# ConvFFN up projection: the summed weight blocks of Strassen's product are formed by adding DMAs instead of by vector instructions, with signs turned

## The chip, the core and the metric

The kernel runs on one core of a Trainium2 chip. Five engines work beside each other, each through its own list of instructions in order: TensorE (PE, matrix products), VectorE (DVE), ScalarE (ACT), GpSimd (POOL) and SyncE (SP, which here only issues DMAs). They wait for each other and for DMAs through semaphores. All DMAs of the core share 16 DMA engines. The metric is the device time of one execution in microseconds (us), as the median over runs.

## The reference

Two decoder layers over 1024 tokens of width 1024. Layer 0 mixes tokens by gated linear attention and layer 1 by native sparse attention, both beside attention to a memory; each layer ends in a ConvFFN. The change lies in the ConvFFN, whose inner width is 2816:

```python
def conv_ffn(h, w_up, conv_w, conv_b, w_down):
    T = h.shape[1]
    a, b = jnp.split(h @ w_up, 2, axis=-1)
    a_pad = jnp.pad(a, ((0, 0), (CONV_WIDTH - 1, 0), (0, 0)))
    a = sum(a_pad[:, j:j + T] * conv_w[j] for j in range(CONV_WIDTH)) + conv_b
    return (jax.nn.silu(a) * b) @ w_down
...
x = x + conv_ffn(rmsnorm(x, g_ffn[l]), w_up[l], conv_w[l], conv_b[l], w_down[l])
```

## The kernel before

Everything is kept transposed: channels on the 128 partitions, tokens along the free dimension. A float32 operand of a product is split into a rounded high part (ACT copies it, `split`, L1022) and a low part, the difference (DVE, L1023). Each product then takes three matmuls (high by high, high by low, low by high: L1058, L1059, L1060).

**Units.** The up projection of a layer is cut into 22 units (`class Up`). Unit i makes 128 channels of the convolved branch a and the same 128 channels of the gate b. Its weights are four blocks of 128 x 512 float32, 256 KB each: block(j, k) with j = 0 for a and 1 for b, and k the half of the 1024 inputs. Called A00, A01, A10, A11 below. The right-hand side, the normalised stream, is also cut into two halves of channels by two halves of 512 tokens. A unit is thus a 2 x 2 by 2 x 2 block product, made by Strassen's scheme (in Winograd's form) with seven products instead of eight. The products are named 1 to 7 (`p1` to `p7`), and each takes 4 x 3 = 12 matmuls of 128 x 128 by 512 columns.

**Left operands.** Products 1, 2 and 4 take A00, A01 and A11 as they are (`direct`). The other four take sums (`sums`, L1042 to L1045): S1 = A10 + A11 for product 5, S3 = A00 - A10 for 7, S2 = S1 - A00 for 6, and S4 = A01 - S2 for 3. For the four first units of a layer these sums run on DVE, for the 18 others on POOL. They are written in place, into the two raw tiles that the four blocks were loaded into (`load`, L1019), and then split by `split67` and `split35`, two blocks to an instruction.

**Right operands.** `blocks1` makes the sums and differences of the normalised stream (L591, L592, L598, L599) once per layer; `h_d` holds one block for later.

**Results.** Products 1, 2 build X (the first token half of a); ACT copies product 1 to s1. Product 6 opens the PSUM bank Y, and DVE reads it at once into q (`opened`, L1092); product 7 adds to the same bank, and DVE reads it into t (`drained`, L1097); product 4 adds to it again (L1106). So PE may start product 7 only when q has been read, and product 4 only when t has been read. Products 5 and 3 use the bank W. The convolution is ACT's L1117 followed by DVE's L1119 and L1123 (called taps below), the gate is a product with silu on DVE, and `mixed` forms the sums that the down projection needs of the gated values (L1147). They are stored to `gb_d`.

**Order.** Per layer: units 0 and 1 run as a pair beside the end of the output projection. Units 2 to 5 are "early" units: their products 1 and 2 are made ahead from separately loaded weights (`pre`) and kept in DRAM, so that they have only products 6, 7, 5, 4, 3 left. After the pair the order is 6, 2, 7, 3, 8, 4, 9, 5 and then 10 to 21: late and early units in turn, later late units alone. `run(u, last, then, after)` writes one step: the products of u, the convolution of the unit before it, the splits of the next unit, the loads of the one after. A scheduler in the framework then sets each engine's order from this. On an early unit's step the product 1 of the next unit is made too, so that in the alternating part every step has six products.

**Buffers.** Four raw tiles of 128 x 1024, two per unit; six tiles for split operands ("wrl") and four pairs for the others ("Ah", "Al").

**Down projection.** `add_x` and the last products add its result to the stream x (L1377, L1465).

Of the kernel before, what the change touches and what calls it, by code (L numbers as in the profile page):

```python
# [14 lines left out]
P = 128  # L15
# [19 lines left out]
def kernel(  # L35
# [543 lines left out]
    def blocks1(norm, gc, B):  # L579
        rs = norm.done()  # L580
        yield "norm"
        lo, hi = xs[:4], xs[4:]
        a, b = hs(0), hs(1)
        tt = nc.vector.tensor_tensor

        for r in (7, 6, 5, 4, 3):
            B[r] = []
        for j in range(4):
            scaled_x(1, rs, gc, (j, 4 + j))
            nc.sync.dma_start(h_d[j], hi[j][:, b])  # L590
            tt(lo[j][:, b], hi[j][:, b], lo[j][:, b], ALU.subtract)  # L591
            tt(lo[j][:, a], lo[j][:, b], lo[j][:, a], ALU.add)  # L592
# [386 lines left out]
    def ffn(l, blocks_, after):  # L979
# [8 lines left out]
        def slot(what, n, make):  # L988
            if what not in ring:
                ring[what] = [make() for _ in range(n)]  # L990
                turn[what] = 0
            turn[what] += 1
            return ring[what][turn[what] % n]

        turn = {}

        def either(n):
            if "A" not in ring:
                ring["A"] = [(V(F32R, "Ah"), V(F32R, "Al")) for _ in range(2)]
            return ring["A"][n]  # L1000

        def raws():
            return [wp.tile([P, 1024], F32, tag="raw", name=nm("wu"), bufs=4) for _ in range(2)]

        class Up:
# [5 lines left out]
            def load(self, k=None):  # L1011
                if k is None:
                    self.load(0)
                    k = 1
                if k == 0:
                    self.raw = slot("raw", 2, raws)
                t = self.raw[k]
                for j in (1, 0) if self.early else (0, 1):
                    nc.sync.dma_start(t[:, hs(j)], w_up[l, j * NF + self.i, :, hs(k)])  # L1019
# [9 lines left out]

            def direct(self):  # L1030
                t = slot("one", 2, lambda: wrl("A"))
                hi, lo = t[:, hs(0)], t[:, hs(1)]
                if self.early:
                    self.split((4,), self.raw[1][:, hs(1)], hi, lo)
                else:
                    self.split((1,), self.raw[0][:, hs(0)], hi, lo)
                    self.split((2, 4), self.raw[1], *slot("two", 2, lambda: (wrl("Ah"), wrl("Al"))))

            def sums(self):
                (a0, b0), (a1, b1) = ((t[:, hs(0)], t[:, hs(1)]) for t in self.raw)  # L1040
                tt = (nc.vector if self.soon else nc.gpsimd).tensor_tensor
                tt(b1, b0, b1, ALU.add)  # L1042
                tt(b0, a0, b0, ALU.subtract)
                tt(a0, b1, a0, ALU.subtract)
                tt(a1, a1, a0, ALU.subtract)  # L1045

            def split67(self, past=None):
                self.split((6, 7), self.raw[0], *either(self.i == 1), past)

            def split35(self, past=None):  # L1050
                self.split((3, 5), self.raw[1], *either(self.i != 0), past)
# [136 lines left out]
        def ahead(then, after):  # L1188
            if after is not None:
                after.load(1)  # L1190
            if then is not None and then.early:
                then.again()

        def run(u, last, then, after):
            nxt = [then] if then is not None else []
            if u.s1 is None:
                u.p1()
            u.p6()
            if after is not None:
                after.load(0)  # L1200
            if u.early:
# [3 lines left out]
                u.split35((then.kept, u.opened))  # L1205
# [23 lines left out]
            mix(u.ended)  # L1229
            u.p3()  # L1230
# [8 lines left out]
        for n, u in enumerate(seq):  # L1239
            u.n, u.mate = n // 2, seq[n - 1] if n % 2 else None  # L1240
            u.soon = n < 4
        each(pair, "load", "direct")
# [4 lines left out]
        each(pair, "sums")  # L1247
# [3 lines left out]
        each(pair, "split67", "p6", "p7")  # L1251
        next(rest)
        each(pair, "act0", "split35", "p5")
# [6 lines left out]
        then.sums()  # L1260
        each(pair, "p3")
        then.split67()
# [155 lines left out]
        def down():  # L1418
# [40 lines left out]
            for t0, w in segs_:  # L1459
                c = slice(t0, t0 + w)  # L1460
                for m in range(4):
# [3 lines left out]
                    tt(xv, bank[m][:, c], xv, ALU.add)  # L1465
# [560 lines left out]
```

## Time and profile before

| | |
|---|---|
| median of 3 runs | 2257.14 us (2255.66 to 2258.51) |
| span of the profiled execution | 2257.4 us; no other time of this execution is given |
| PE busy | 2215.0 us, 98% |
| DVE busy | 1729.8 us, 77% |
| ACT busy | 1126.3 us, 50% |
| POOL busy | 433.6 us, 19%, of it 212.0 us in the sums L1042 to L1045 |
| DMA | 285.15 MB, mean 126 GB/s |

The page gives busy time per engine, the chain that ended last, and groups of instructions with the idle time in front of them. PE's share alone tells that there is little idle time to win; where the 42 us lie in which PE is idle, the windows and the table of waits tell. Times in the rows are from the start of the span; layer 0's up projection stands at about 400 to 840 us, layer 1's at about 1630 to 2030 us.

### The profile page before, as it was taken

The page shows a single profiled execution, that of the slowest core. Times are in us where ns is not written, and L with a number is a line of the kernel's source. Part 1 is how long each engine was busy: PE and PEld are TensorE (multiplying, and loading weights), DVE is VectorE, ACT ScalarE, POOL GpSimd, SP SyncE. Part 2 cuts the span into 40 slices and gives each one's busy share as a digit, 9 for nine tenths or more (in the row PEclk, how much of TensorE's full clock was granted, in tenths as well). Part 3 has the DMA queues.
Part 4 walks back from the last instruction along what each step waited for, and adds up shares of the span by engine and source line. Part 5 has one row for each costly group of instructions (what it writes and reads, how often), then busy time and mean ns, then how long its engine had stood idle before and what let it go on. Part 6 is the DMA issues. An engine that isn't in the chain of part 4 may idle for free.

```text
span 2257.4 us, 31218 instructions
## 1 busy us (share of the span) xinstructions
PE 2215.0 (98%) x10994; PEld 1826.2 (81%) x10994; DVE 1729.8 (77%) x3069; ACT 1126.3 (50%) x2085; POOL 433.6 (19%) x409
## 2 busy tenths in 40 slices
PE   9999999999999999999999999999999999999997
PEld 7888887777888888888888878778777788888886
DVE  6786886888877768887756778866988877768877
ACT  5464464543333335456544788864543333334445
POOL 1222300013333210000103334420013333210000
PEclk9999999999999999999999999999999999999999
DMA  6332246333332329544421111036433333329533
GB/s 227 103 104 87 73 161 208 138 126 133 129 122 98 108 84 345 173 135 136 131 83 50 40 46 37 8 115 206 140 130 131 126 122 103 108 76 339 167 96 112
DMA packets 139451, 285.15 MB, mean 126 GB/s; under 512 B 16221, under 2 KB 22958, under 8 KB 139294
## 3 DMA queue, kind: packets, MB, share of 16 engines
q1 hardware_dynamic: 130942, 263.11, 35.5%
q0 software_dynamic: 3600, 11.65, 1.5%
q10 hardware_dynamic: 4752, 8.39, 1.0%
q8 instruction: 86, 1.41, 0.3%
q14 instruction: 71, 0.58, 0.1%
HBM read 211.27 MB, written 71.83 MB: 125 GB/s over the span
## 4 chain that ended last, share of the span: by engine, by line
PE 78%; DVE 10%; ACT 4%; DMA 4%; issue 2%; SPq 0%; POOL 0%; DVEq 0%; ACTq 0%; POOLq 0%
PE dn L1413 5%; PE dn L1414 5%; PE dn L1412 5%; PE fy L1058 5%; PE fy L1060 5%; PE fy L1059 5%; PE fx L1058 3%; PE fx L1059 3%; PE fx L1060 3%; PE fw L1060 3%; PE fw L1059 3%; PE fw L1058 3%; PE op L195 2%; PE op L196 2%; PE op L194 2%
## 5 line engine op out<-in xcount | busy, mean ns | idle before, releaser
L1413 PE MATMUL dn<-db,da 128*128 128x512 f32 (+1 forms) x628 | 242.5, 386 | 0.6 <-DVE db L1342 0.5
L1412 PE MATMUL dn<-db,da 128*128 128x512 f32 (+1 forms) x628 | 242.6, 386 | 0.2 <-ACT db L1341 0.2
L1414 PE MATMUL dn<-db,da 128*128 128x512 f32 (+1 forms) x628 | 241.7, 385 | 0.0
L1058 PE MATMUL fy<-B,Ah 128*128 128x512 f32 x496 | 194.6, 392 | 10.8 <-DVE q L1092 9.9
L1060 PE MATMUL fy<-B,Al 128*128 128x512 f32 x496 | 193.3, 390 | 0.4 <-DVE Al L1023 0.4
L1059 PE MATMUL fy<-B,Ah 128*128 128x512 f32 x496 | 193.1, 389 | 0.0
L1042 POOL TENSOR_TENSOR wu<-wu,wu 128x512 f32<-128x512 f32 x36 | 47.2, 1311 | 735.1 <-DVE Al L1023 600.5
L1022 ACT ACTIVATE Ah<-wu 128x1024 fp32r<-128x1024 f32 x124 | 130.4, 1052 | 102.8 <-PE fy L1059 60.3
L1023 DVE TENSOR_TENSOR Al<-wu,Ah 128x1024 fp32r<-128x1024 f32 x124 | 160.8, 1297 | 8.4 <-ACT Ah L1022 7.3
L1413 PEld LDWEIGHTS dn<-db,da 128*128 128x128 f32 x628 | 117.9, 188 | 26.8 <-DVE db L1342 2.8
L1412 PEld LDWEIGHTS dn<-db,da 128*128 128x128 f32 x628 | 118.0, 188 | 24.4 <-ACT db L1341 0.6
L1060 PE MATMUL fw<-B,Al 128*128 128x512 f32 x352 | 137.7, 391 | 0.0
L1058 PE MATMUL fw<-B,Ah 128*128 128x512 f32 x352 | 137.1, 390 | 0.0
L1059 PE MATMUL fw<-B,Ah 128*128 128x512 f32 x352 | 137.1, 389 | 0.0
L1414 PEld LDWEIGHTS dn<-db,da 128*128 128x128 f32 x628 | 117.9, 188 | 23.2
L1342 DVE TENSOR_TENSOR db<-bl,db 128x512 fp32r<-128x512 f32 x154 | 106.0, 688 | 28.4 <-ACT db L1341 27.9
L1058 PEld LDWEIGHTS fy<-B,Ah 128*128 128x128 f32 x496 | 93.1, 188 | 35.2 <-DVE q L1092 14.1
L1341 ACT ACTIVATE db<-bl 128x512 fp32r<-128x512 f32 x154 | 95.7, 621 | 31.3 <-PE dn L1414 20.6
L1060 PEld LDWEIGHTS fy<-B,Al 128*128 128x128 f32 x496 | 93.1, 188 | 20.6 <-DVE Al L1023 0.9
L1059 PEld LDWEIGHTS fy<-B,Ah 128*128 128x128 f32 x496 | 93.1, 188 | 18.9
L1138 ACT ACTIVATE fc<-fc 128x512 f32<-128x512 f32 x88 | 54.9, 626 | 106.3 <-DVE fc L1119 85.2
L1341 ACT ACTIVATE da<-wb 128x512 fp32r<-128x512 f32 x88 | 54.9, 628 | 101.4 <-PE dn L1413 63.9
(416 smaller groups left out, 6185.8 us busy)
## 6 DMA issues: line engine op xcount, KB each, us to landing
wu<-in_w_up_dram SPq DMA_DIRECT2D x176, 256.0 KB, 3.0
bl<-gb_d SPq DMA_DIRECT2D x154, 256.0 KB, 2.9
gb_d<-fc SPq DMA_DIRECT2D x132, 256.0 KB, 2.4
wb<-in_w_down_dram SPq DMA_DIRECT2D x44, 256.0 KB, 4.2
wa<-in_w_down_dram SPq DMA_DIRECT2D x22, 512.0 KB, 7.8
wo<-in_a_wo_dram SPq DMA_DIRECT2D x16, 512.0 KB, 3.7
xre<-om_d SPq DMA_DIRECT2D x32, 256.0 KB, 4.3
x_r<-x SPq DMA_DIRECT2D x32, 256.0 KB, 2.4
```

The lines of the kernel that those rows point to most:

```text
L1022: a = nc.scalar.activation(hi, src, AF.Copy)
L1023: b = nc.vector.tensor_tensor(lo, src, f(hi), ALU.subtract)
L1042: tt(b1, b0, b1, ALU.add)
L1058: mm(ps, wr, hr, start=(first and j == 0), stop=False, skip_group_check=True)
L1059: mm(ps, wr, hl, start=False, stop=False, skip_group_check=True)
L1060: mm(ps, wl, hr, start=False, stop=(stop and j == 3), skip_group_check=True)
L1138: silu[0] = nc.scalar.activation(self.c[half], self.c[half], AF.Silu)
L1341: nc.scalar.activation(w[:, hs(0)], t, AF.Copy)
L1342: b = tt(w[:, hs(1)], t, f(w)[:, hs(0)], ALU.subtract)
L1412: mm(o, hi, bh, start=first, stop=False, skip_group_check=True)
L1413: mm(o, hi, bl, start=False, stop=False, skip_group_check=True)
L1414: mm(o, lo, bh, start=False, stop=stop or n == NP - 1, skip_group_check=True)
```

## The change

The signs of A10 and A11 are turned in thought, so that all sums of weights become plain additions: A00 + A10 for product 7, A10 + A11 for 5, T = A00 + A10 + A11 for 6, and T + A01 for 3. The gate b then comes out negated, and so do the gated values and the whole down projection. To make this right, three kinds of right-hand blocks are formed with the sign turned (`neg_sub`, a scalar_tensor_tensor in the place of a tensor_tensor), and the results of the down projection are subtracted from x.

The sums themselves are made by DMAs issued on POOL that load a block from DRAM and add it to what lies in SBUF (`accum_op`). The raw tiles are laid out anew: R (two tiles in turn, one a unit) holds A00 and A11; Q and T (one tile each, a half to a unit) hold A01 and A00. A unit has four plain loads on SP (an early unit three, without Q) and five adding loads on POOL: T + A10, then T + A11, both halves of R + A10, and, once product 6's operand is split, T + A01. The second addition to T waits for the first to land. The splits are regrouped: 1 and 4 together, 7 and 5 together (`split75`), and 2, 6 and 3 alone. The instructions L1042 to L1045 are gone from DVE and POOL.

```diff
+        def neg_sub(o, p, q):
+            nc.vector.scalar_tensor_tensor(o, p, -1.0, q, ALU.mult, ALU.subtract)
...
-            tt(lo[j][:, a], lo[j][:, b], lo[j][:, a], ALU.add)
+            neg_sub(lo[j][:, a], lo[j][:, b], lo[j][:, a])
...
-            tt(lo[j][:, b], hi[j][:, b], lo[j][:, a], ALU.subtract)
-            tt(hi[j][:, a], hi[j][:, a], lo[j][:, a], ALU.subtract)
+            neg_sub(lo[j][:, b], hi[j][:, b], lo[j][:, a])
+            neg_sub(hi[j][:, a], lo[j][:, a], hi[j][:, a])
...
+            def load(self):
+                self.load_r()
+                self.load_q()
+                self.sum_t(0)
+                self.sum_t(1)
+
+            def load_r(self):
+                self.place()
+                nc.sync.dma_start(self.R[:, hs(0)], self.block(0, 0))
+                nc.sync.dma_start(self.R[:, hs(1)], self.block(1, 1))
+
+            def load_q(self):
+                if not self.early:
+                    nc.sync.dma_start(self.Q, self.block(0, 1))
+                nc.sync.dma_start(self.T, self.block(0, 0))
+
+            def more(self, t, j, k):
+                nc.gpsimd.dma_start(t, self.block(j, k), accum_op=ALU.add)
+
+            def sum_t(self, k):
+                self.more(self.T, 1, k)
+
+            def sum_r(self):
+                for h in range(2):
+                    self.more(self.R[:, hs(h)], 1, 0)
+
+            def sum_s4(self):
+                self.more(self.T, 0, 1)
...
-            def sums(self):
-                (a0, b0), (a1, b1) = ((t[:, hs(0)], t[:, hs(1)]) for t in self.raw)
-                tt = (nc.vector if self.soon else nc.gpsimd).tensor_tensor
-                tt(b1, b0, b1, ALU.add)
-                tt(b0, a0, b0, ALU.subtract)
-                tt(a0, b1, a0, ALU.subtract)
-                tt(a1, a1, a0, ALU.subtract)
...
+                    self.split((1, 4), self.R, hi, lo)
+                    self.one(2, self.Q, "Z3" if self.pos == 1 else "Z2")
...
             u.p6()
-            if after is not None:
-                after.load(0)
+            each(two, "load_r")
...
-                u.split35((u.kept, u.opened))
+                u.split3((u.kept, u.opened))
                 ahead(then, after)
                 u.p7()
                 each(nxt, "direct")
             u.act0()
-            each(nxt, "sums")
+            each(nxt, "sum_r")
             u.p5()
             mix(u.summed)
             for v in nxt:
-                v.split67((u.acted, u.drained))
+                v.split6((u.acted, u.drained))
+                v.sum_s4()
+            for v in two:
+                v.sum_t(0)
+                v.sum_t(1)
...
             u.p4()
             mix(u.ended)
+            each(nxt, "split75")
             u.p3()
...
-            tt(xv, ps, xv, ALU.add)
+            tt(xv, xv, ps, ALU.subtract)
```

`ahead` now calls `load_q` for the unit after the next. Two places in the order of the built program matter below. On POOL there stand before, at units 3 and 8 of layer 0, the in-place sums, four to a unit (the four raw tiles are wu_639 to wu_642):

```order
L1042 TENSOR_TENSOR wu_640_3520<-wu_639_3519,wu_640_3520 128x512 [waits DMAHW7_49,DMAHW6_49,DVE_49]
L1043 TENSOR_TENSOR wu_639_3519<-wu_639_3519 128x512 [waits DMAHW0_49,Pool_49]
L1044 TENSOR_TENSOR wu_639_3519<-wu_640_3520,wu_639_3519 128x512 [waits Pool_49]
L1045 TENSOR_TENSOR wu_640_3520<-wu_640_3520,wu_639_3519 128x512 [waits DMAHW7_49,Pool_49]
L1042 TENSOR_TENSOR wu_642_3522<-wu_641_3521,wu_642_3522 128x512 [waits DMAHW6_49,DMAHW4_49,DVE_49]
L1043 TENSOR_TENSOR wu_641_3521<-wu_641_3521 128x512 [waits DMAHW2_49,Pool_49]
```

Now POOL issues adding loads there. In the changed kernel wu_641 is T, wu_639 and wu_642 are the two tiles R. The rows are, one after the other: T of unit 8 + A10, T of unit 8 + A11, T of unit 3 + A01, both halves of R of unit 8, a half of R of unit 4, T of unit 4 + A10, T of unit 4 + A11, T of unit 8 + A01, and the other half of R of unit 4:

```order
L1038 DMA wu_641_3521<-in_w_up_dram 128x512 [waits DMAHW5_49,DMASW4_49]
L1038 DMA wu_641_3521<-in_w_up_dram 128x512 [waits DMASW5_49,DMASW4_49]
L1038 DMA wu_641_3521<-in_w_up_dram 128x512 [waits DMASW6_49,DMASW1_49,DVE_49]
L1038 DMA wu_639_3519<-in_w_up_dram 128x512 [waits DMAHW3_49,DMASW7_49,DVE_49]
L1038 DMA wu_639_3519<-in_w_up_dram 128x512 [waits DMAHW4_49]
L1038 DMA wu_642_3528<-in_w_up_dram 128x512 [waits DMAHW3_49]
L1038 DMA wu_641_3521<-in_w_up_dram 128x512 [waits DMAHW0_49,DMASW2_49]
L1038 DMA wu_641_3521<-in_w_up_dram 128x512 [waits DMASW3_49,DMASW2_49]
L1038 DMA wu_641_3521<-in_w_up_dram 128x512 [waits DMASW5_49,DVE_49]
L1038 DMA wu_642_3528<-in_w_up_dram 128x512 [waits DMAHW4_49,DVE_49]
```

So the addition that makes unit 8's operand for product 3 (the last row but one) stands behind unit 4's second addition to T, which waits for unit 4's first addition (the last wait named, DMASW2, is that one's completion), which waits for unit 4's load of T.

On DVE, at unit 8 (a late unit), from the reading of Y after product 6 (q_763) to its reading after product 7 (t_769), there stands before:

```order
L1092 TENSOR_TENSOR q_763_4573<-fy_762_4560,s1_755_4474 128x512
L1023 TENSOR_TENSOR Al_695_3825<-wu_642_3522,Ah_694_3824 128x1024
L1119 SCALAR_TENSOR_TENSOR fc_765_4591<-fx_754_4461,cs_69,fc_765_4591 128x511
L1119 SCALAR_TENSOR_TENSOR fc_766_4595<-q_753_4453,cs_69,fc_766_4595 128x511
L1119 SCALAR_TENSOR_TENSOR fc_765_4591<-fx_754_4461,cs_69,fc_765_4591 128x510
L1123 SCALAR_TENSOR_TENSOR fc_766_4595<-edge_758_4502,cs_69,fc_766_4595 128x1
L1119 SCALAR_TENSOR_TENSOR fc_766_4595<-q_753_4453,cs_69,fc_766_4595 128x510
L1123 SCALAR_TENSOR_TENSOR fc_766_4595<-edge_758_4502,cs_69,fc_766_4595 128x2
L1097 TENSOR_TENSOR t_769_4623<-fy_762_4560,s1_755_4474 128x512
```

and now:

```order
L1120 TENSOR_TENSOR q_763_4593<-fy_762_4580,s1_755_4492 128x512
L1052 TENSOR_TENSOR A_648_3540<-wu_641_3521,A_648_3540 128x512
L1052 TENSOR_TENSOR A_647_3539<-wu_640_3520,A_647_3539 128x512
L1147 SCALAR_TENSOR_TENSOR fc_765_4611<-fx_754_4479,cs_69,fc_765_4611 128x511
L1147 SCALAR_TENSOR_TENSOR fc_766_4615<-q_753_4471,cs_69,fc_766_4615 128x511
L1147 SCALAR_TENSOR_TENSOR fc_765_4611<-fx_754_4479,cs_69,fc_765_4611 128x510
L1151 SCALAR_TENSOR_TENSOR fc_766_4615<-edge_758_4519,cs_69,fc_766_4615 128x1
L1147 SCALAR_TENSOR_TENSOR fc_766_4615<-q_753_4471,cs_69,fc_766_4615 128x510
L1151 SCALAR_TENSOR_TENSOR fc_766_4615<-edge_758_4519,cs_69,fc_766_4615 128x2
L1125 TENSOR_TENSOR t_769_4643<-fy_762_4580,s1_755_4492 128x512
```

In the place of the split of two blocks out of raw tile 642 stand two splits of one block each: unit 8's operand for product 3 out of T (A_648 from wu_641), and the next late unit's operand for product 2 out of Q. The first of them now needs the adding load shown last but one on POOL; the taps and t stand behind it.

More of the change, by code (lines that the diff above doesn't have):

```diff
@@ L986, in ffn, with area, raws @@
         ring = {}
-        def slot(what, n, make):
+        def area(what):
+            if not ring:
+                for k in "X0 X1 X2 X3 Z2 Z3".split():
+                    ring[k] = wrl("A")
             if what not in ring:
[L990 to L1003, printed above, removed]
+                for k in "Y0 Y1 Z6 Z7".split():
+                    ring[k] = V(F32R, "Ah")
+            return ring[what]
+        def raws(what):
+            if what not in ring2:
+                ring2[what] = wp.tile([P, 1024], F32, tag="raw", name=nm("wu"), bufs=4)
+            return ring2[what]
+        ring2 = {}
         class Up:
@@ L1009, in __init__, with block, place @@
                 self.s1 = None
[L1011 to L1019, printed above, removed]
+            def block(self, j, k):
+                return w_up[l, j * NF + self.i, :, hs(k)]
+            def place(self):
+                n = self.pos % 2
+                self.R = raws(f"R{n}")
+                self.Q, self.T = (raws(k)[:, hs(n)] for k in "QT")
+            def load(self):
[20 more added lines that the diff above has]
+                self.more(self.T, 0, 1)
             def split(self, keys, src, hi, lo, past=None):
@@ L1028, in split, with one, split75, split6 @@
                     self.A[key] = hi[:, hs(j)], lo[:, hs(j)]
+            def one(self, key, src, to, past=None):
+                t = area(to)
+                self.split((key,), src, t[:, hs(0)], t[:, hs(1)], past)
             def direct(self):
[L1031 to L1032 removed]
+                hi, lo = (area(f"X{2 * (self.pos % 2) + j}") for j in range(2))
                 if self.early:
[L1034 removed]
+                    self.split((4,), self.R[:, hs(1)], hi[:, hs(1)], lo[:, hs(1)])
                 else:
[L1036 to L1051 removed]
+                    self.split((1, 4), self.R, hi, lo)
+                    self.one(2, self.Q, "Z3" if self.pos == 1 else "Z2")
+            def split75(self, past=None):
+                hi, lo = (area(k) for k in (("Z2", "Z3") if self.pos == 1 else ("Y0", "Y1")))
+                self.split((7, 5), self.R, hi, lo, past)
+            def split6(self, past=None):
+                self.one(6, self.T, "Z7" if self.pos % 2 else "Z6", past)
+            def split3(self, past=None):
+                self.one(3, self.T, ("Z6", "Z7")[self.pos] if self.pos < 2 else "Z3", past)
             def product(self, ps, r, first, stop):
@@ L1189, in ahead @@
             if after is not None:
-                after.load(1)
+                after.load_q()
             if then is not None and then.early:
@@ L1195, in run @@
             nxt = [then] if then is not None else []
+            two = [after] if after is not None else []
             if u.s1 is None:
@@ L1204, in run @@
                 each(last, "end")
-                u.split35((then.kept, u.opened))
+                u.split3((then.kept, u.opened))
                 ahead(then, after)
@@ L1239, in ffn @@
         for n, u in enumerate(seq):
-            u.n, u.mate = n // 2, seq[n - 1] if n % 2 else None
-            u.soon = n < 4
-        each(pair, "load", "direct")
+            u.pos, u.n, u.mate = n, n // 2, seq[n - 1] if n % 2 else None
+        each(pair, "load", "direct", "sum_r")
         each(pair, "p1")
@@ L1250, in ffn @@
         next(rest)
[L1251 removed]
+        each(pair, "split6", "split75", "sum_s4", "p6", "p7")
         next(rest)
[L1253 removed]
+        each(pair, "act0", "split3", "p5")
         next(rest)
@@ L1259, in ffn @@
         then.direct()
-        then.sums()
+        then.sum_r()
         each(pair, "p3")
-        then.split67()
+        then.split6()
+        then.sum_s4()
+        then.split75()
         last = pair
@@ L1464, in down @@
                     xv = xs[m][:, HT + t0 : HT + t0 + w]
-                    tt(xv, bank[m][:, c], xv, ALU.add)
+                    tt(xv, xv, bank[m][:, c], ALU.subtract)
                     norm = nn[[e[0] for e in ends].index(HT + t0)]
```

1 line of the change is left out of this document (removed).

## Prediction

> **What bounds the kernel now.** I read the page's shares first, then the windows over the up projections, then the table of waits, and last the timelines of DVE and POOL where PE waits. The page, and one row of the waits of the whole span (waits in us in total, times, longest):
>
> ```profile
> span 2257.4 us, 31218 instructions
> PE 2215.0 (98%) x10994; PEld 1826.2 (81%) x10994; DVE 1729.8 (77%) x3069; ACT 1126.3 (50%) x2085; POOL 433.6 (19%) x409
> PE fy L1058 <- DVE q L1092: 9.9, 7, 2.7
> ```
>
> PE is the bound, and the change leaves its matmuls as they are. It can only take away or add idle time of PE. Where that lies in the two up projections, the windows show (length, then busy time and instructions of PE, PEld, DVE, ACT, POOL; granted clock; DMA share; GB/s):
>
> ```profile
> 440.00:460.00 20.00, 18.04 (x76) 13.59 (x75) 19.44 (x31) 13.37 (x22) 0.00 (x0) 1.00 0.38 130
> 500.00:530.00 30.00, 26.90 (x117) 21.61 (x116) 24.97 (x39) 12.62 (x18) 5.48 (x5) 1.00 0.40 140
> 620.00:630.00 10.00, 9.31 (x42) 7.37 (x41) 9.38 (x14) 4.28 (x7) 2.90 (x2) 1.00 0.37 119
> 1630.00:1640.00 10.00, 9.31 (x41) 7.41 (x40) 9.86 (x15) 7.96 (x14) 0.00 (x0) 1.00 0.48 158
> 1680.00:1710.00 30.00, 25.98 (x114) 20.84 (x113) 25.20 (x34) 9.67 (x14) 10.92 (x7) 1.00 0.35 123
> 1770.00:1780.00 10.00, 8.65 (x38) 6.84 (x37) 7.68 (x11) 3.37 (x6) 5.47 (x4) 1.00 0.33 101
> 1800.00:1820.00 20.00, 19.29 (x85) 15.64 (x84) 18.39 (x24) 9.46 (x13) 6.44 (x4) 1.00 0.37 107
> 640.00:840.00 200.00, 200.00 (x884) 165.62 (x883) 142.92 (x200) 69.50 (x104) 51.49 (x37) 1.00 0.27 94
> ```
>
> In the first seven PE is idle for 1.96 + 3.10 + 0.69 + 0.69 + 4.02 + 1.35 + 0.71 = 12.5 us. From 640 us on, where only late units follow each other, it isn't idle at all. So the change can win 12.5 us at most, 0.55%. The first and fourth window (2.65 us) are the start of a layer, where right-hand blocks are made; the other five hold the 9.9 us of the row of waits. All these waits are one kind: product 7 adds to the bank Y, and must wait until DVE has read product 6 out of it (q).
>
> Why DVE is late, its timeline before one such wait shows (start, duration, line, instruction), with two rows of POOL beside it:
>
> ```profile
> 493.61 1.72 DVE L1023 TENSOR_TENSOR Al<-wu,Ah 128x1024 fp32r<-128x1024 f32 x1
> 495.26 1.77 DVE L1119 SCALAR_TENSOR_TENSOR fc<-q,cs,fc 128x511 f32<-128x511 f32 x1
> 496.95 1.24 DVE L1123 SCALAR_TENSOR_TENSOR fc<-edge,cs,fc 128x1 f32<-128x1 f32 x1
> 506.33 1.22 DVE L1023 TENSOR_TENSOR Al<-wu,Ah 128x1024 fp32r<-128x1024 f32 x1
> 494.33 2.15 POOL L1043 TENSOR_TENSOR wu<-wu 128x512 f32<-128x512 f32 x1
> 496.56 1.62 POOL L1044 TENSOR_TENSOR wu<-wu,wu 128x512 f32<-128x512 f32 x1
> ...
> 520.44 1.76 DVE L1023 TENSOR_TENSOR A<-wu,A 128x512 fp32r<-128x512 f32 x1 [2.29 <-ACT A L1022]
> ```
>
> While POOL sums, DVE instructions are stretched: the split takes 1.72 us at 493.61 and 1.22 at 506.33, a tap over one column takes 1.24. And at 520.44 DVE idles 2.29 us for ACT, whose block had been loaded late. The Trainium skill ("SBUF — State Buffer", section "Who interferes with whom") says that a DVE instruction with two inputs in SBUF and a GpSimd instruction that reads SBUF block each other as a whole; these rows agree.
>
> **The change part by part.** *Removed: the sums.* 144 instructions on POOL and 32 on DVE go, and so does the stretching. The blocks of product 2 and of R also get a tile of their own, so that they are loaded a step earlier. I take all 9.9 us of q waits as gone: -9.9. If only the stretched ones went, and not those behind a late load, it would be some half of it.
>
> *Added: signs.* 24 tensor_tensor become scalar_tensor_tensor, 12 per layer, and these lie in the first and fourth window, where DVE is busy 19.44 of 20 and 9.86 of 10 us:
>
> ```profile
> 435.69 0.75 DVE L566 SCALAR_TENSOR_TENSOR x<-x,cs,rs 128x512 f32<-128x512 f32 x1
> 436.35 0.69 DVE L592 TENSOR_TENSOR x<-x 128x512 f32<-128x512 f32 x1
> ```
>
> That is 24 x 0.06 = 1.4 us, all on the path at worst: +1.4, and 0 at best. The subtraction in the down projection is the same instruction with other operands: nothing. One split more per unit (two of one block for one of two) lies on ACT and DVE, at 50% and 77%: hidden, and where it isn't, it is counted in the chain below.
>
> *Added: 220 adding loads on POOL, and a chain.* Here the gain can be lost. In the alternating part the operand of product 3 of a late unit is made by the addition of A01 to T. On POOL that stands behind the early unit's second addition, which waits for the first to land. So the chain is: the split that frees the early unit's half of T, its load, an addition (X), a second addition (X), and queued behind that the late unit's addition of A01. Then ACT's split, DVE's split, one more split, the taps and t; only when t has been read may PE start product 4. The rows of the parts (groups: count, busy us, mean ns; taps from the timeline; DMA rows: count, size, us to landing):
>
> ```profile
> L1082 ACT ACTIVATE s<-fx 128x512 f32<-128x512 f32 x44 | 26.0, 591 | 99.3 <-PE fx L1060 99.2
> L1117 ACT ACTIVATE fc<-q,cs 128x512 f32<-128x512 f32 x44 | 35.6, 810 | 0.8 <-DVE q L1112 0.8
> L1022 ACT ACTIVATE A<-wu 128x512 fp32r<-128x512 f32 x44 | 27.7, 629 | 101.8 <-PE fx L1059 78.8 <-DMA wu<-in_w_up_dram 16.2 <-PE op L196 4.1
> ...
> 524.34 0.74 DVE L1119 SCALAR_TENSOR_TENSOR fc<-fx,cs,fc 128x511 f32<-128x511 f32 x1
> 525.00 0.73 DVE L1119 SCALAR_TENSOR_TENSOR fc<-q,cs,fc 128x511 f32<-128x511 f32 x1
> 525.66 0.74 DVE L1119 SCALAR_TENSOR_TENSOR fc<-fx,cs,fc 128x510 f32<-128x510 f32 x1
> 526.32 0.20 DVE L1123 SCALAR_TENSOR_TENSOR fc<-edge,cs,fc 128x1 f32<-128x1 f32 x1
> 526.44 0.74 DVE L1119 SCALAR_TENSOR_TENSOR fc<-q,cs,fc 128x510 f32<-128x510 f32 x1
> 527.10 0.21 DVE L1123 SCALAR_TENSOR_TENSOR fc<-edge,cs,fc 128x2 f32<-128x2 f32 x1
> 527.23 0.68 DVE L1097 TENSOR_TENSOR t<-fy,s 128x512 f32<-128x512 f32 x1
> ...
> wu<-in_w_up_dram SPq DMA_DIRECT2D x176, 256.0 KB, 3.0
> x<-in_x_dram POOLq DMA_DIRECT2D x4, 512.0 KB, 6.2
> xre<-in_x_dram POOLq DMA_DIRECT2D x8, 256.0 KB, 4.3
> ...
> DMA to landing us min/median/max: 3.1/4.3/5.9
> ...
> q0 software_dynamic: 3600, 11.65, 1.5%
> ```
>
> The cover is counted from the end of product 1 of the late unit. PE then makes 7, 5, 4, 3 of the early unit and 6, 2, 7, 5 of the late one: 8 products of 12 matmuls. With 200.00 us for 884 matmuls (0.226 each) that is 21.7 us. Against it stand:
> - before the load: ACT's copy s 0.59, ACT's first step of the convolution 0.81, two long and two short taps (by the starts 0.66 and 0.12 each) 1.6, the split's DVE half 0.7: 3.7
> - the load of T: 3.0
> - two additions: 2X
> - the late unit's addition, which moves its bytes after the second one's. Queue q0 moved 11.65 MB in 1.5% of 16 engines' 2257.4 us, so 344 GB/s, 0.76 us for 256 KB. An addition reads two streams, its source and what it adds to; at twice the time this is 1.5
> - behind it: ACT's split 0.63, two DVE splits 0.69 + 0.60, and from 524.34 to the end of t at 527.91, 3.6: 5.5
>
> In sum 13.7 + 2X against 21.7: each late unit waits 2X - 8.0, and nothing if X is below 4.0. There are 8 such units (7, 8, 9 and 10 in each layer). Before the first of each layer's, 4 of the 12 matmuls of product 2 now stand in front of product 6, so its cover is 8 matmuls or 1.8 us shorter: 3.6 more for both layers.
>
> The additions to R stand on POOL beside this chain. They land about X + 1.5 after issue and have 4 products, 10.9 us, until product 7 needs their split, which takes twice 0.63 on ACT and 1.22 on DVE (below X = 6.9 this is hidden). Behind POOL's waits nothing else is queued in this stage; behind T's load on SP stand stores and loads for later steps, for which nobody waits within the step.
>
> X, the time from issue to landing of an adding load, no row shows. Lower end: a plain load of the size on POOL's queue at its fastest, 3.1 us (xre). Upper end: 6.2 us, the loads of twice the bytes (x). Between them lie 3.1 with the second stream added, 3.1 + 0.76 = 3.9, and the median of the plain loads with it, 4.3 + 0.76 = 5.1. Additions come two and three at a time and beside SP's loads, so I expect neither the fastest nor the median, and take X = 4.7, roughly the middle of these two (an estimate). Then a late unit waits 1.4 us.
>
> The sum: -9.9 + 1.4 + 8 x 1.4 + 3.6 = +6.3 us. The span of 2257.4 us, which is all that is known of the profiled execution, stands 0.3 above the median of the runs, 2257.14. From the median, 2263.4; I forecast **2264 us**. In general the change is 16X - 68.9 us for X above 4.0. About 0.2%, 4.5 us, is what a measurement of this kernel can tell from no change.
>
> **The rivals.** *Faster: the additions land in time.* If X stays below 4.0, the chain fits under the 8 products, save for the first late unit of each layer. This decides at X = 4.02, where the formula passes -4.5 us. For it speaks the 3.9 of above; against it the median of 4.3 without any addition. At X = 3.9 both first units still wait 1.6: -9.9 + 1.4 + 3.2 = -5.3, 2252 us; at 3.1 nothing waits, -8.5, 2249 us. The Trainium skill ("Collectives: The Full Stack", "The bandwidth ceiling: the fold count and why AG ≠ RS ≠ AR") says that the adding in a DMA is itself free and that the second source read halves the rate. By that rule X would be 3.9 and the time 2252; no trace so far shows an addition.
>
> *No change that can be measured.* X between 4.02 and 4.6: the waits for q are replaced by waits for t of the same sum, 2253 to 2262 us.
>
> *Much slower: additions crowd the DMA engines.* If one takes as long as 6.2 us, the formula gives +30, 2287 us; the loads of SP, at a DMA share of 0.27 to 0.48 now, would land later too, and more splits than the one of product 3 would wait. It is part of the slower case.
>
> *The stretching was not the cause.* If DVE is as late without POOL's sums, because late loads hold it, perhaps half of the 9.9 us stay, and the time is 2269. Speaks for it the idle 2.29 at 520.44; against it that the split there is itself stretched to 1.76 us.
>
> **How the numbers follow.** X = 4.7 and above 4.6: 0.5, of it 0.1 above 5.9. Between: 0.25. Below 4.02: 0.25. The forecast is that of the likeliest case, whose own range is 2262 to 2292 us. The range over all reaches from 2249 (X = 3.1) to 2292 (X = 6.2, and some us for what else would then wait). Faster 0.25, same 0.25, slower 0.5.
>
> **What would show it.** Adding loads on POOL's queue with a median landing of 4.7 us; DVE splits of 1024 columns at 1.22 us throughout; no row of PE waiting for q; instead PE fy waiting for t of L1125, about 1.4 us each time, in 8 places, with ACT A L1051 waiting for an adding load in front of each. The late units from 640 us on stay without idle time. I am wrong if X lands outside 4.6 to 5.9; if PE waits for t though the additions land below 4.0, since then the cover is miscounted; or if PE waits in the part from 640 us on.

## The result, and the profile after

The changed kernel takes 2280.88 us (median of 4 runs, 2278.87 to 2286.8) beside 2257.34 us of the kernel before (median of 4 runs): a ratio of 1.0106, 95% interval 1.009 to 1.0122. It is slower by 1.06%, 23.5 us. The forecast was 2264 us with a range of 2249 to 2292. In two of the kernels below one execution took far longer than the others (3699 and 7865 us); their medians are those of the other executions.

The page of the changed kernel, its first lines:

```profile
span 2280.9 us, 31693 instructions
PE 2220.1 (97%) x10994; PEld 1832.9 (80%) x10994; DVE 1660.1 (73%) x3081; ACT 1133.8 (50%) x2129; POOL 412.7 (18%) x485
```

The span grew by 23.5 us. PE is now idle for 2280.9 - 2220.1 = 60.8 us, where it was 2257.4 - 2215.0 = 42.4: 18.4 us more. The other 5.1 us are in PE's busy time, with the same 10994 matmuls. So there are two things to explain. The table of waits of the changed kernel (us in total, times, longest):

```profile
PE fy L1086 <- DVE t L1125: 22.0, 8, 5.2
PE fx L1086 <- ACT s L1110: 4.7, 6, 1.7
PE fy L1088 <- DVE Ah L1052: 1.8, 2, 0.9
```

The row of waits for q, 9.9 us before, is gone. In its place stand 8 waits for t, as forecast in kind and number, but of 22.0 us and not 14.8. The waits for s (PE may refill a bank only when ACT has copied it) were 1.4 us before:

```profile
PE fx L1058 <- ACT s L1082: 1.4, 2, 0.7
```

The windows show the place; the first two are windows that the forecast used:

```profile
500.00:530.00 30.00, 26.10 (x115) 21.11 (x113) 18.39 (x31) 8.55 (x15) 6.02 (x7) 0.98 0.76 188
640.00:840.00 200.00, 200.00 (x884) 165.60 (x883) 134.64 (x210) 73.19 (x114) 43.13 (x51) 1.00 0.73 169
525.00:531.30 6.30, 1.11 (x6) 0.57 (x4) 4.94 (x10) 4.06 (x8) 0.76 (x1) 0.79 0.59 179
531.30:535.30 4.00, 4.00 (x9) 3.13 (x10) 3.48 (x5) 1.22 (x3) 0.08 (x1) 0.50 0.81 188
569.70:573.00 3.30, 3.30 (x9) 2.59 (x8) 2.88 (x4) 1.02 (x2) 0.17 (x1) 0.50 0.94 223
1731.40:1737.00 5.60, 5.60 (x13) 4.36 (x14) 3.56 (x6) 1.84 (x4) 1.93 (x3) 0.50 0.70 181
1771.10:1774.50 3.40, 3.40 (x9) 2.63 (x8) 2.40 (x4) 0.59 (x1) 1.62 (x2) 0.50 0.77 208
```

DVE has air now (18.39 us of 30, before 24.97; in part because it waits itself), and the late units from 640 us on still run without a gap, though the DMA share there rose from 0.27 to 0.73. The third row is the longest wait for t: PE works 1.11 us of 6.30. The last four rows are what nobody had in the sum: behind each of the four longest waits the granted clock is 0.50 for 3.3 to 5.6 us, while PE is busy without a gap. That is 16.3 us at half speed, so 8.2 us lost.

The additions themselves, in the rows of DMA issues (count, size, median us to landing) and of queue q0:

```profile
q0 software_dynamic: 35280, 69.33, 17.2%
...
wu<-in_w_up_dram POOLq DMA_DIRECT2D x220, 256.0 KB, 6.3
wu<-in_w_up_dram SPq DMA_DIRECT2D x168, 256.0 KB, 3.6
```

An addition lands 6.3 us after its issue in the median, where 4.7 had been expected, and SP's plain loads take 3.6 us instead of 3.0. How the median is made up, the chain in front of the longest wait shows: the chain of waits first, then the timelines of POOL, ACT and DVE (in brackets the idle time in front, and what ended it).

```profile
509.75 2.51 DMA wu<-in_w_up_dram
512.80 0.84 POOL wu L1038
513.64 4.16 issue
```

```profile
512.80 0.84 POOL L1038 DMA_DIRECT2D wu<-in_w_up_dram  x1 [7.19 <-DMA wu<-in_w_up_dram]
517.81 2.60 POOL L1038 DMA_DIRECT2D wu<-in_w_up_dram  x3 [4.17 <-DMA wu<-in_w_up_dram]
...
525.70 1.15 ACT L1051 ACTIVATE A<-wu 128x512 fp32r<-128x512 f32 x2 [11.08 <-DMA wu<-in_w_up_dram]
...
530.56 0.68 DVE L1125 TENSOR_TENSOR t<-fy,s 128x512 f32<-128x512 f32 x1
```

Unit 3's half of T is loaded from 509.75 on and its first addition issued at 512.80 (3.05 us). At 517.81, 5.0 us later, that one has landed, and POOL issues three in a row: unit 3's second addition, unit 7's addition of A01, and one to R. ACT waits 11.08 us for A01, until 525.70, which is 7.9 us after the second addition's issue. Then DVE's splits and taps, and t. By the completion events in the trace the second addition landed at 524.3, 6.5 us after its issue, and A01 1.3 us behind it.

The 23.5 us put together:

| | us |
|---|---|
| waits for q gone | -9.9 |
| waits for t | +22.0 |
| waits for s (1.4 to 4.7) | +3.3 |
| other idle time of PE (18.4 less the three above) | +3.0 |
| half clock behind the four longest waits for t | +8.2 |
| other busy time of PE (5.1 less 8.2) | -3.1 |

The last row has no cause shown. It isn't the clock: summed over the windows of the whole span, half clock cost PE 3.4 us before (two stretches, at 10 and 75 us) and 11.7 now, of it 8.3 in the up projections. Two profiled executions of one and the same kernel below differ by as much, PE being busy 2210.3 and 2207.1 us, but 1.7 us of that is a stretch at half clock (at 74 us) that only the first one has.

### The profile page after: what moved, and what is told of

The parts are those of the page before. It is cut to its first block, busy times and chain, and to the rows that moved or that the text cites. A ratio compares the mean times of both kernels' runs of the same rounds, so it can differ in the third digit from the quotient of the medians.

```text
span 2280.9 us, 31693 instructions
## 1 busy us (share of the span) xinstructions
PE 2220.1 (97%) x10994; PEld 1832.9 (80%) x10994; DVE 1660.1 (73%) x3081; ACT 1133.8 (50%) x2129; POOL 412.7 (18%) x485
## 3 DMA queue, kind: packets, MB, share of 16 engines
q0 software_dynamic: 35280, 69.33, 17.2%
## 4 chain that ended last, share of the span: by engine, by line
PE 70%; DVE 12%; DMA 6%; ACT 6%; issue 5%; POOL 1%; SPq 0%; DVEq 0%; POOLq 0%; ACTq 0%
PE dn L1445 5%; PE dn L1446 5%; PE dn L1447 5%; PE fy L1086 4%; PE fy L1088 4%; PE fy L1087 4%; PE fx L1086 3%; PE fx L1088 3%; PE fx L1087 3%; DMA wu<-in_w_up_dram 3%; PE fw L1086 3%; PE fw L1088 3%; PE fw L1087 3%; PE op L195 2%; PE op L194 2%
## 5 line engine op out<-in xcount | busy, mean ns | idle before, releaser
L1038 POOL DMA_DIRECT2D wu<-in_w_up_dram x220 | 190.5, 1020 | 809.5 <-DMA wu<-in_w_up_dram 644.6
L1051 ACT ACTIVATE A<-wu 128x512 fp32r<-128x512 f32 (+1 forms) x122 | 92.2, 763 | 233.9 <-DMA wu<-in_w_up_dram 84.1
L1052 DVE TENSOR_TENSOR A<-wu,A 128x512 fp32r<-128x512 f32 (+1 forms) x122 | 103.6, 854 | 83.3 <-ACT A L1051 79.9
L1088 PE MATMUL fy<-B,Ah 128*128 128x512 f32 x344 | 134.1, 390 | 1.8 <-DVE Ah L1052 1.8
L1086 PE MATMUL fy<-B,Ah 128*128 128x512 f32 x344 | 133.9, 389 | 0.0
L1087 PE MATMUL fy<-B,Ah 128*128 128x512 f32 x344 | 133.8, 389 | 0.0
L1086 PE MATMUL fx<-B,A 128*128 128x512 f32 x288 | 113.1, 393 | 3.0 <-ACT s L1110 3.0
L1110 ACT ACTIVATE s<-fx 128x512 f32<-128x512 f32 x44 | 26.0, 596 | 174.3 <-PE fx L1088 174.3
L1088 PE MATMUL fx<-B,A 128*128 128x512 f32 x288 | 112.1, 389 | 0.0
L1087 PE MATMUL fx<-B,A 128*128 128x512 f32 x288 | 112.1, 389 | 0.0
L1120 DVE TENSOR_TENSOR q<-fy,s 128x512 f32<-128x512 f32 x44 | 30.4, 691 | 107.0 <-PE fy L1088 98.4
L194 PE MATMUL op<-om,wor 128*128 128x512 f32 x256 | 101.7, 398 | 0.5 <-ACT om L230 0.5
L195 PE MATMUL op<-om,wor 128*128 128x512 f32 x256 | 100.0, 391 | 0.7 <-DVE om L231 0.7
```

What stands on the lines that cost most here:

```text
L194: mm(ps, wr[:, k, :], hr, start=(k == 0), stop=False)
L195: mm(ps, wr[:, k, :], hl, start=False, stop=False)
L1038: nc.gpsimd.dma_start(t, self.block(j, k), accum_op=ALU.add)
L1052: b = nc.vector.tensor_tensor(lo, src, f(hi), ALU.subtract)
L1086: mm(ps, wr, hr, start=(first and j == 0), stop=False, skip_group_check=True)
L1087: mm(ps, wr, hl, start=False, stop=False, skip_group_check=True)
```

## The experiments

The theory after the result: unit 7's addition of A01 is late because it is queued behind an addition that waits for another one to land; long waits of PE then also cost clock. The main rival: the additions are slow because too many are under way at once, and their order doesn't matter.

**Order alone.** On POOL, each unit's addition of A01 is fixed ahead of the second addition to T of the unit that follows it. No byte more or less is moved.

```diff
             for v in two:
                 v.sum_t(0)
-                v.sum_t(1)
+                t1 = v.sum_t(1)
+                for w in nxt:
+                    follow(t1, w.s4, "order")
```

> The changed kernel, with one order fixed on POOL: a unit's addition of A01 is issued ahead of the next-but-one unit's second addition to T. Theory (the late unit's A01 addition is late because it is queued behind an addition that waits for another one to land): the 22.0 us of PE waiting for t vanish (under 3 us left), the granted clock does not fall to a half there, and the time falls from 2281 to 2249 to 2257 us. Rival (adding loads are slow because too many are in flight at once): the order moves no bytes, the waits for t stay above 12 us and the time above 2268 us.

Measured: 2254.22 us, ratio to before 0.999 (0.9979 to 1.0002). The waits of PE, and the timelines of POOL and ACT at the same place:

```profile
PE fx L1086 <- ACT s L1110: 4.8, 6, 1.4
...
PE fy L1086 <- DVE t L1125: 0.4, 2, 0.2
```

```profile
512.32 0.84 POOL L1038 DMA_DIRECT2D wu<-in_w_up_dram  x1 [7.17 <-DMA wu<-in_w_up_dram]
515.07 0.85 POOL L1038 DMA_DIRECT2D wu<-in_w_up_dram  x1 [1.91 <-DVE Ah L1052]
517.24 1.72 POOL L1038 DMA_DIRECT2D wu<-in_w_up_dram  x2 [1.32 <-DMA wu<-in_w_up_dram]
...
520.23 1.15 ACT L1051 ACTIVATE A<-wu 128x512 fp32r<-128x512 f32 x2 [6.09 <-PE fx L1088]
```

A01 is now issued at 515.07, as soon as the split that reads T is done; by the completion events it landed at 520.15, and ACT splits it at 520.23 instead of 525.70 (the profile puts the end of that wait down to PE, which was done 0.1 us later). The 22.0 us of waits for t became 0.4. In this execution the granted clock has no stretch at a half in the up projections. The queue's order was the cause of the waits, and the rival falls as the main cause: the additions still take 6.0 us in the median to land. The whole loss is won back by a change that moves nothing else.

The same kernel was run once more, beside the gated one below.

> The kernel with A01 ahead of the second addition once more, on the same chip as the gated one, for the comparison: 2252 to 2257 us, ratio to before 0.998 to 1.000; waits for t under 1 us again.

Measured: 2252.11 us, ratio 0.998 (0.9968 to 0.9993), waits for t 1.1 us. It is a little faster than the kernel before, by much less than the 9.9 us of q would let one hope: the waits for s (4.3 us) and the other small ones of the changed kernel are still there.

**Plain loads in place of adding ones.**

```diff
-                nc.gpsimd.dma_start(t, self.block(j, k), accum_op=ALU.add)
+                nc.gpsimd.dma_start(t, self.block(j, k))
```

> The changed kernel with its 220 adding loads issued as plain loads in the same order on every engine; the sums are thus left out. Theory (an in-chain addition takes about 5 us because it reads a second stream): landing falls from a median of 6.3 us to 3 to 4.3 us, the chain fits under the products, waits for t are 0 to 3 us, 2250 to 2258 us. Rival (it is POOL's issuing and its queue that are slow, not the adding): landing stays above 5 us, waits for t stay above 12 us, time above 2268 us.

Measured: 2255.32 us, ratio 0.9992 (0.998 to 1.0004). The DMA rows and the waits:

```profile
q0 software_dynamic: 21200, 69.33, 10.0%
...
wu<-in_w_up_dram POOLq DMA_DIRECT2D x220, 256.0 KB, 4.0
```

```profile
PE fy L1086 <- DVE t L1125: 2.8, 3, 1.4
```

With the median of 4.0 us as X the forecast's formula leaves 3.6 us of waits for t; with 3.4 us, the mean of the sixteen loads of the chain by the trace's completion events, it leaves 1.2. Measured were 2.8, between the two. So the count of the cover was right to some 2 us, and adding is what lengthens X. Its price comes from q0: 69.33 - 11.65 = 57.7 MB took 10.0 - 1.5 = 8.5% of this span of 2246.7 us as plain loads (302 GB/s), and in the changed kernel 15.7% of 2280.9 us as additions (161 GB/s).

**Without the additions to R.** `sum_r` does nothing.

> The changed kernel without the 88 additions to R; products 7 and 5 thus get unsummed weights. Theory (the chain through T alone makes the waits; an addition takes about 5 us by itself): the waits for t stay at 15 to 22 us, the time at 2272 to 2281 us. Rival (the additions crowd each other): landing falls below 4.5 us, waits for t below 5 us, 2252 to 2262 us.

Measured: 2273.31 us, ratio 1.0061 (1.0043 to 1.0079). The DMA row and the waits:

```profile
wu<-in_w_up_dram POOLq DMA_DIRECT2D x132, 256.0 KB, 4.7
```

```profile
PE fy L1085 <- DVE t L1124: 15.2, 8, 3.8
```

Both sides have a part. Most of the waits stay, as the theory says; landing falls to 4.7, not quite below the rival's 4.5, and the waits for t fall by 6.8 us. The 88 additions to R thus make 6.8 of the 22.0 us, the chain through T the other 15.2. Whether they do it by sharing the DMA engines or by their place in POOL's queue, this run doesn't tell apart. The waits for s, 4.7 us in the changed kernel, are back at their size of before:

```profile
PE fx L1085 <- ACT s L1109: 1.4, 2, 0.7
```

**The second addition twice.** In the steps of early units the second addition to T is issued twice, and the late unit's addition of A01 behind both.

```diff
+                if v.early:
+                    t1 = v.sum_t(1)
+                    for w in nxt:
+                        w.sum_s4()
+                        follow(w.s4, t1, "order")
```

> The changed kernel with the second addition to T of the three early units of the alternating part issued twice, ahead of the late unit's A01 addition (A11 thus counts twice there). Theory (each addition in the chain costs its own landing time, about 5 us, and every late unit already waits): the 6 late units in whose step this happens wait 5 us more each, +30 us; and since PE idles over 3 us in each of these places, the granted clock falls to a half behind each, about +2 us per place, +12 us: 2315 to 2330 us. Without the effect on the clock 2306 to 2314 us. Rival (crowding, not the chain): under +12 us.

Measured: 2314.66 us, ratio 1.025 (1.0235 to 1.0264), 33.8 us above the changed kernel.

```profile
span 2311.8 us, 31695 instructions
PE 2224.8 (96%) x10994; PEld 1835.5 (79%) x10994; DVE 1661.8 (72%) x3081; ACT 1133.9 (49%) x2129; POOL 417.8 (18%) x491
```

```profile
PE fy L1086 <- DVE t L1125: 35.5, 6, 10.6
PE fy L1086 <- ACT Ah L1051: 13.3, 2, 7.1
```

PE idles 87.0 us, 26.2 more, which is 4.4 us for each of the 6 places and not quite the 5 expected. The two waits put down to ACT's split Ah are at two of the same six places (6.3 us at 611 and 7.1 at 1741). PE's busy time rose by 4.7 us more, where 12 had been expected: four of the six places had their half clock in the changed kernel already. In the up projections half clock now costs 15.9 us, where it cost 8.3. The total of 2314.66 lies just below the range expected with an effect on the clock (2315 to 2330) and just above the one without (2306 to 2314), so that it alone wouldn't decide on the clock. Crowding alone (under 12 us) is ruled out.

**Before, without POOL's sums.** `sums` returns at once for all but the four first units.

> The kernel before without its sums on POOL (the 18 later units of each layer split the unsummed blocks); loads, splits and matmuls are as before. Theory (POOL's sums stretch DVE, and that makes the waits for q): the 9.9 us of PE waiting for q fall below 2 us, DVE's splits of 1024 columns all take 1.22 us, PE idles about 32 us instead of 42. Rival (the waits for q come from blocks loaded late, and not from the stretching): 4 us or more of waits for q stay.

Measured: 2248.33 us, ratio 0.9952 (0.9939 to 0.9965). No row of PE waiting for q is left, and PE idles 2249.0 - 2211.8 = 37.2 us, not 32: other waits of a microsecond differ from run to run. DVE at the place of the forecast's stretched rows, and where it idled for a late block:

```profile
493.78 1.22 DVE L1023 TENSOR_TENSOR Al<-wu,Ah 128x1024 fp32r<-128x1024 f32 x1
495.57 0.22 DVE L1125 SCALAR_TENSOR_TENSOR fc<-edge,cs,fc 128x1 f32<-128x1 f32 x1
...
518.58 0.69 DVE L1023 TENSOR_TENSOR A<-wu,A 128x512 fp32r<-128x512 f32 x1 [2.04 <-ACT A L1022]
```

1.22 where it was 1.72, 0.22 where it was 1.24. The blocks were loaded as late as before (DVE still idles 2.04 us for ACT there, before 2.29), so POOL's sums were the cause of all the waits for q. This is also what the change could have won: 10 us.

**The signs alone.** In the kernel before, the 24 instructions become scalar_tensor_tensor with a factor of 1.0.

```diff
+        def stt(o, p, q, op):
+            nc.vector.scalar_tensor_tensor(o, p, 1.0, q, ALU.mult, op)
...
-            tt(lo[j][:, a], lo[j][:, b], lo[j][:, a], ALU.add)
+            stt(lo[j][:, a], lo[j][:, b], lo[j][:, a], ALU.add)
```

> The kernel before with the 24 instructions of the right-hand blocks as scalar_tensor_tensor with the factor 1.0, so that only the price of the instruction changes. Theory of the forecast (0.06 us each, all on the path at worst): PE's idle time at the start of the two layers grows from 2.7 us by up to 1.4 us, and the time by less than can be measured, 2255 to 2260 us beside the 2257 of before. Rival (hidden): no growth of the idle time.

Measured: 2256.22 us, ratio 0.9988 (0.9979 to 0.9997). DVE's timeline, and the window of the layer's start:

```profile
434.95 0.75 DVE L566 SCALAR_TENSOR_TENSOR x<-x,cs,rs 128x512 f32<-128x512 f32 x1
435.61 0.69 DVE L587 SCALAR_TENSOR_TENSOR x<-x 128x512 f32<-128x512 f32 x1
```

```profile
440.00:460.00 20.00, 18.04 (x75) 13.57 (x74) 19.54 (x32) 12.40 (x21) 0.00 (x0) 1.00 0.41 145
```

The signs cost nothing: with a constant factor the instruction takes 0.69 us like the tensor_tensor before, in the changed kernel too; the 0.75 that the forecast used belongs to a factor read from a column of `cs`. PE's 18.04 us are those of before.

**What makes s late.** At the start of a layer ACT splits the separately loaded weights of units 2 to 5 (`wa`, 512 KB each), and waits for them. Their median landing, before and in the changed kernel:

```profile
wa<-in_w_up_dram SPq DMA_DIRECT2D x8, 512.0 KB, 3.9
```

```profile
wa<-in_w_up_dram SPq DMA_DIRECT2D x8, 512.0 KB, 6.7
```

The first try took it for SP's queue, where unit 6's load of A01 waits for a split ahead of the third of these loads; it was put behind the last.

```diff
-                    nc.sync.dma_start(self.Q, self.block(0, 1))
+                    q = nc.sync.dma_start(self.Q, self.block(0, 1))
+                    if self.pos == 2:
+                        follow(q, us[PRE - 1].wa, "order")
```

> The kernel with A01 ahead of the second addition, and also the load of unit 6's A01 put behind the last load of the separately loaded weights on SP, where it waits for a split and holds up these. Theory (that wait on SP makes ACT late at the start of a layer, and so PE waits for s): the 4.8 us of PE fx waiting for ACT s fall below 2.5 us, the time to 2250 to 2254 us. Rival (those loads are late because adding loads share the DMA engines with them): the waits for s stay above 3.5 us.

Measured: 2257.15 us, ratio 0.9992 (0.9979 to 1.0005), landing 7.6 us, and:

```profile
PE fx L1088 <- ACT s L1112: 7.9, 6, 3.5
```

This theory fell: the waits for s did not shrink. The rival of that run, that additions share the DMA engines with these loads, was tried next. Four small ACT instructions per layer, behind the last of the splits, read what the additions will write, and so hold the first two units' second additions and their additions to R back:

```diff
+            def gate(self, past):
+                for src in (self.T[:, :2], self.R[:, HT - 1 : HT + 1]):
+                    g = S([P, 2], s="gate", bufs=2)
+                    follow(nc.scalar.activation(g, src, AF.Copy), past, "order")
+                self.sum_t(1)
+                self.sum_r()
...
+        for v in pair:
+            v.gate(us[PRE - 1].high)
```

> The kernel with A01 ahead of the second addition, where the first two units' second additions to T and additions to R are issued only after ACT has split the last separately loaded weights (8 of these 512 KB loads in all; four small ACT instructions per layer hold the additions back). Theory (adding loads in flight beside these loads make them land late, 7.4 us in the median instead of 3.9, and PE then waits for ACT's s): they land in under 5.5 us, the waits for s fall from 4.8 to under 2 us, and the time is 2 to 3 us below that of the kernel without the gate, 2249 to 2254 us beside 2257 of before. Rival (the loads land late for another reason, such as where they stand on SP): landing stays above 6.5 us and the waits for s above 3.5 us.

Measured: 2264.94 us, ratio 1.0037 (1.0024 to 1.005): worse. The waits, and ACT's timeline behind the gate:

```profile
PE fx L1093 <- ACT s L1117: 15.8, 5, 7.4
```

```profile
439.21 1.06 ACT L1058 ACTIVATE A<-wu 128x1024 fp32r<-128x1024 f32 x1 [7.64 <-DMA wu<-in_w_up_dram]
440.17 0.58 ACT L1117 ACTIVATE s<-fx 128x512 f32<-128x512 f32 x1
```

The loads did land earlier, 5.7 us in the median and a little above what was expected. But ACT's queue held one split of a summed block, of unit 1, ahead of a copy s; it now waits 7.64 us for the additions held back, and s behind it. It is the mistake of the change itself on another queue. So the first two units' splits of summed blocks were put behind these copies as well:

```diff
-        each(pair, "split6", "split75", "sum_s4", "p6", "p7")
+        past = us[PRE - 2].kept, us[PRE - 1].low
+        for v in pair:
+            v.split6(past)
+        for v in pair:
+            v.split75(past)
+        each(pair, "sum_s4", "p6", "p7")
```

> The gated kernel, with the first two units' splits of summed blocks (products 6, 7 and 5) put behind the copies s of the separately loaded units on ACT. Theory (the gated kernel lost 15.8 us of waits for s because a split of a summed block stood in ACT's queue ahead of s; without it the gate leaves what the earlier landing gains): the waits for s fall from 15.8 us below 2.5, the separately loaded weights land in under 6 us, 2249 to 2254 us, ratio to before 0.996 to 0.999. Rival (the additions held back are then late for products 6 and 7 of the first units, 10 us further on): a wait of over 3 us for one of their splits appears, and the time is above 2256 us.

Measured: 2247.10 us, ratio 0.9954 (0.9936 to 0.9972).

```profile
span 2242.2 us, 31691 instructions
PE 2208.1 (98%) x10994; PEld 1825.3 (81%) x10994; DVE 1661.4 (74%) x3081; ACT 1134.5 (51%) x2137; POOL 412.8 (18%) x485
```

```profile
PE fx L1093 <- ACT s L1117: 1.6, 3, 0.7
```

```profile
wa<-in_w_up_dram SPq DMA_DIRECT2D x8, 512.0 KB, 5.3
```

The waits for s are back at their size of before (1.6 us), none for a split of the first units appears, and PE idles 34.1 us in the profiled execution (2244.02 us) instead of 42.4. This version beats both kernels: 10 us below the one before, 34 below the changed one, and it is faster than the 2249 to 2254 us expected. Both runs with the gate speak for the crowding: the 512 KB loads landed at 5.7 and 5.3 us instead of 6.7 to 7.6. So do two runs above: without the additions to R they landed at 5.3 us and the waits for s were 1.4 us; with plain loads in place of the additions it was 5.9 and 1.7. How much of the gain is the gate's and how much the later splits' was not tried apart.

## Why the prediction was right, and where its sizes failed

The direction, the place and the mechanism were right, and 2281 lies in the range. The sum was +6.3 us and the result +23.5, and that the range still holds it is in part luck: its upper end stands for additions of 6.2 us in the chain, which did not come. Of the 17.2 us that the sum lacks, 7.2 are waits for t; the rest is made of terms that it doesn't have: half clock (+8.2), waits for s (+3.3) and other idle time (+3.0), less the signs (1.4) and PE's other busy time (3.1). By its steps:

- **"I take all 9.9 us of q waits as gone."** Right, and for the reason given: without POOL's sums they vanish. The rival by which late loads were the cause falls.
- **Signs, +1.4.** Nothing. The price was taken from a row with a column factor.
- **The chain, 8 waits of 2X - 8.0 and 3.6 for the first ones.** Right in form: for the plain loads it gives 1.2 to 3.6 us, and 2.8 were measured. Worked back from the waits, it gives X = 5.15 with 22.0 us, and 4.73 without the additions to R. The completion events in the trace of the changed kernel put it otherwise: the sixteen additions of the chain took 4.75 us in the mean (3.7 to 6.5), so X = 4.7 was right, and the terms beside X were too small. POOL issued the second addition 0.3 us after the first had landed, for which the sum has nothing; A01 landed 1.8 us behind the second addition in the mean and not 1.5; and ACT began 0.1 us later still. With the 0.1 of X that is 0.8 us a unit, of the 0.9 that are missing. What also failed is the sentence that the additions to R "stand on POOL beside this chain": without them the waits were 6.8 us less. At unit 7 the terms were: load 3.05 us (forecast 3.0), first addition 5.0 (4.7), from the second addition's issue to A01's landing 7.9 (4.7 + 1.5). Together 2.0 us more, and the wait is 5.2 us where 3.2 were forecast. Here it was the second addition that took long (6.5 us).
- **"It can only take away or add idle time of PE."** This step failed. Behind its four longest waits PE works at half clock: +8.2 us.
- **The start of a layer.** The chain was placed in the alternating part only. That four additions of each of the first two units meet the 512 KB loads was not looked at: waits for s, +3.3 us.
- **"The late units from 640 us on stay without idle time."** Right.
- **What would show it.** DVE's splits at 1.22 us, no wait for q, 8 waits for t behind ACT's L1051: all seen. (At unit 8 of both layers the profile puts ACT's wait down to PE, which was done within 0.1 us behind the landing of the addition.) The median landing of 4.7 us was wrong (6.3), which lies outside the 4.6 to 5.9 that the prediction named as its own limit; only the mean of the chain's additions (4.75) lies inside. Most additions are issued two and three at a time, and those issued last in such a group land last (7.3 and 8.1 us in the group at 517.81).

The Trainium skill ("Collectives: The Full Stack", "The bandwidth ceiling: the fold count and why AG ≠ RS ≠ AR") tells of the additions of ring collectives that the adding is free and the second source read halves the rate. The measured 161 against 302 GB/s agree (a factor of 1.9). X still grew by more than the 0.76 us that the forecast's rival took for it: from 3.4 to 4.75 us in the chain, and from 4.0 to 6.3 in the median over all.

## What to carry to other kernels

A sum made by an adding DMA is off the vector engines, but not off the queues: each addition to a block waits here for the one before it, and everything issued behind it on that engine waits too. So issue first what is ready and due, and hold back what isn't due; here the order on two queues turned a loss of 1.06% into a gain of 0.46%. When a wait of PE is priced, add the clock: in these up projections a gap of 2.9 us or more always cost another 1.7 us or more, and a gap of 2.0 to 2.7 us sometimes did.

## What the runs showed of the hardware that was not expected

**A wait of PE that costs twice.** Every gap of PE of 2.9 us or more in the up projections of these traces is followed by a granted clock of 0.50 while PE is already busy again, 3.3 us or longer: at least 1.7 us lost for each. Shorter gaps do it at times: one of 2.46 us did in the run without additions to R, one of 2.15 in the changed kernel did not. In the run with the second addition twice, a gap of 2.0 us (first row) has its 3.4 us at half clock (second row); in the kernel before, one of 2.7 us has not (last two rows):

```profile
652.00:654.50 2.50, 0.50 (x3) 0.24 (x2) 2.50 (x7) 1.71 (x4) 0.69 (x1) 1.00 0.37 130
655.60:659.00 3.40, 3.40 (x10) 2.61 (x9) 2.50 (x4) 0.78 (x1) 0.82 (x2) 0.51 0.89 230
```

```profile
1687.50:1690.50 3.00, 0.33 (x3) 0.01 (x1) 3.00 (x6) 1.83 (x3) 0.00 (x0) 1.00 0.80 298
1690.50:1696.00 5.50, 5.50 (x24) 4.57 (x25) 5.12 (x9) 1.88 (x3) 0.00 (x0) 1.00 0.42 146
```

The Trainium skill ("TensorE: Matmul & The Clock Gate", "What's actually happening") tells of an activity window of 3413 ns that runs freely, by which the clock is halved or restored. The 3.4 us at half clock agree, and so does that gaps of like length count or not, if it depends on where in the window they fall. Its section "Why this matters for your kernels" puts the limit at gaps of about 3 us; here 2.0 us were enough once. Gaps aren't the only occasion: in the kernel before, the clock falls to 0.50 at 75.1 us for 3.4 us though PE was busy without a gap in the 7 us ahead; why, no run here shows.

**Adding DMAs.** 161 GB/s against 302 for plain loads of the same blocks in the same order. The trace has each addition as 128 packets of 2048 bytes, 178 ns each in the median, and each plain load as 64 packets of 4096 bytes at 159 ns; so the rate halves with the size of the packets, and whether the second read or the smaller packets cost the time, no run here tells apart. POOL also takes longer to issue one: 0.84 us in the rows of POOL above, 0.54 as a plain load:

```profile
450.37 0.54 POOL L1038 DMA_DIRECT2D wu<-in_w_up_dram  x1 [20.05 <-DVE Ah L1052]
```
